# Rotating a matrix by 90 degrees: the last macro tile's outputs as 1024 by 512 blocks, and five loads issued ahead

## The chip, the cores and the metric

One core of one Trainium2 chip. The metric is the device time of one execution in microseconds. A profiled execution also has a span, from its first to its last instruction, which is a little shorter than its device time.

## The reference

```python
x = np.random.randn(8192, 8192).astype(np.float32)
def reference(x, k):        # k = 1
    return np.rot90(x, k)
```

Nothing is calculated. Column c of `x` becomes row 8191 - c of the output: the matrix is transposed and its rows are put in reverse order. 268 MB are read and 268 MB are written.

## The kernel before

The input is cut into 16 macro tiles of 1024 rows (R) by 4096 columns (W). A macro tile is loaded as 8 row tiles (T) of 128 rows by 4096 columns, 2 MB each: loads 8 kk to 8 kk + 7 for macro tile kk, 128 in all. It is stored as 8 outputs (J), 128 in all; output n = 8 kk + j holds the 512 columns of chunk j over all 1024 rows, which are 512 rows by 1024 columns of the result. A store is 2 MB too: each of 128 partitions writes four runs (G = 4) of 1024 floats, 4 KB each.

The way of a row tile:

- SP issues its load (`load`, L143) into a landing buffer. Five buffers take the first loads. From load 8 on two of them are for landing (LAND) and three for outputs (OUTS). SP waits until the load before in the same buffer has been copied away.
- DVE copies it into a ring of 63 chunks (SLOTS), reversing the 512 columns of each chunk on the way (L190). A copy is cut into pieces, because the ring is one chunk smaller than a macro tile: piece by piece it waits for the transposes of the macro tile before (`s_half`, `s_first`). Each piece adds one to `s_rev`.
- PE transposes 128x128 blocks of the ring into PSUM (L219), 32 for one output: four blocks times eight row tiles. PSUM is held as two halves, `ps0` and `ps1`, each of 128 x 2048 floats. The first output of a macro tile goes through its row tiles in order, so that PE can start while loads are still coming; the others go through it block by block.
- ACT copies each half from PSUM to an output buffer (L253) and adds one to `s_ev`, for which PE's next use of that half waits. After the second half it issues the store (L259).

Every engine goes through its list in order. `out_buf(n)` gives the buffer of an output: the three output buffers in turn, but for the last eight outputs the two landing buffers are used too, since no more loads come into them. Output 120 takes the buffer of load 126, output 124 that of load 127, output 125 that of load 126 again. ACT waits until the store before in this buffer has landed, or, where a landing buffer is taken for the first time, until its last load has been copied away.

The five engines' programs stand in a block (`nc.Block()`), one function for each. At the end SP waits for all stores.

Of the kernel before, what the change touches and what calls it, by code (L numbers as in the profile page):

```python
# [6 lines left out]
P = 128  # L7


R = 1024  # L10
T = R // P
W = 4096
G = 4
J = W // (G * P)
# [3 lines left out]
CH = G * P  # L18
F = G * R
SLOTS = T * J - 1  # L20

H = 2
GH = G // H
LAND = 2
OUTS = 3

# [19 lines left out]
def slot(kk, t, j):  # L46

    at = t * J + j if kk % 2 == 0 else J + t + j * T
    return (at + kk // 2 * (J + 1)) % SLOTS


def kernel(tc: tile.TileContext, x: bass.AP, k: bass.AP, out: bass.AP):
    nc = tc.nc
# [3 lines left out]
    N, M = x.shape  # L57
    dt = x.dtype
    macros = [(r0, c0) for r0 in range(0, N, R) for c0 in range(0, M, W)]
    KK = len(macros)  # L60
    n_out = KK * J
    n_load = KK * T
    assert T == J


    order = [(kk, a, b) for kk in range(KK) for a in range(T) for b in range(J)]
    for i, (kk, t, j) in enumerate(order):
        if i >= SLOTS:
# [3 lines left out]
    with tc.tile_critical():  # L72
        ident = nc.alloc_sbuf_tensor("ident", [P, P], dt)
        scratch = nc.alloc_sbuf_tensor("scratch", [P, 1], dt)
        bufs = [nc.alloc_sbuf_tensor(f"buf{i}", [P, F], dt) for i in range(LAND + OUTS)]
        ring = nc.alloc_sbuf_tensor("ring", [P, SLOTS * CH], dt)
        ps = [
            nc.alloc_psum_tensor(f"ps{h}", [P, GH * R], mybir.dt.float32)
            for h in range(H)
        ]  # L80

# [3 lines left out]
        s_rev = nc.alloc_semaphore("s_rev")  # L85
        s_first = nc.alloc_semaphore("s_first")
        s_half = nc.alloc_semaphore("s_half")
        s_ev = nc.alloc_semaphore("s_ev")

        def load_buf(m):  # L90
            return m % (LAND + OUTS) if m < T else m % LAND
# [12 lines left out]
        pieces, rev = {}, {}  # L104
        done = 0
        for m in range(n_load):
            kk, t = divmod(m, T)
            got = []
            if m >= T:
                full = (s_half, H * (m - T + 1))  # L110
                first = (s_first, m - T + 2)
            else:
                full = None
                first = (s_first, 1) if t == T - 1 else None
            cuts = [0, 1, J - 1, J] if t == T - 1 else [0, J - 1, J]
            if m < T - 1:
                cuts = [0, J]
            for lo, hi in zip(cuts[:-1], cuts[1:]):
                got.append((lo, hi, first if hi == J else full if lo == 0 else None))
                done += 1  # L120
                for j in range(lo, hi):
                    rev[m, j] = done
            pieces[m] = got
# [16 lines left out]
        def load(e, m):  # L140
            r0, c0 = macros[m // T]
            b = load_buf(m)
            e.dma_start(  # L143
                out=bufs[b][:], in_=x[r0 + m % T * P : r0 + (m % T + 1) * P, c0 : c0 + W]
            ).then_inc(s_land[b], 16)

        def uses_before(n_or_m, buf):
            return sum(buf(i) == buf(n_or_m) for i in range(n_or_m))

        with nc.Block() as block:  # L150

            @block.gpsimd
            def _(e):
                e.memset(ident[:], 0.0).then_inc(s_id, 1)  # L154
                e.wait_ge(s_id, 1)
                e.affine_select(  # L156
                    out=ident[:],
                    in_=ident[:],
                    compare_op=mybir.AluOpType.not_equal,
                    fill=1.0,  # L160
                    base=0,
                    pattern=[[-1, P]],
                    channel_multiplier=1,
                ).then_inc(s_id, 1)

            @block.sync
            def _(e):
                for m in range(n_load):
                    last = [i for i in range(m) if load_buf(i) == load_buf(m)]
                    if last:  # L170
                        e.wait_ge(s_rev, rev[last[-1], J - 1])
                    load(e, m)
                for b in range(LAND + OUTS):
                    n = sum(out_buf(i) == b for i in range(n_out))
                    if n:
                        e.wait_ge(s_store[b], 16 * n)

            @block.vector
            def _(e):
                for m in range(n_load):  # L180
                    kk, t = divmod(m, T)
                    b = load_buf(m)
                    a = bufs[b][:].rearrange("p (j c) -> p j c", c=CH)
                    e.wait_ge(s_land[b], 16 * (uses_before(m, load_buf) + 1))
                    for lo, hi, wait in pieces[m]:
                        if wait:
                            e.wait_ge(*wait)
                        for j, n, at, step in runs(kk, t, lo, hi):
                            v = ring[:, at * CH : (at + (n - 1) * step + 1) * CH]
                            i = e.tensor_copy(  # L190
                                out=bass.AP(
                                    tensor=v.tensor,
                                    offset=v.offset,
                                    ap=[v.ap[0], [step * CH, n], [1, CH]],
                                ),
                                in_=a[:, j : j + n, ::-1],
                            )
                        i.then_inc(s_rev, 1)

            @block.tensor  # L200
            def _(e):
                seen = {}

                def wait(sem, n):
                    if seen.get(sem, 0) < n:
                        seen[sem] = n
                        e.wait_ge(sem, n)

                e.wait_ge(s_id, 2)
                for n in range(n_out):  # L210
                    kk, j = divmod(n, J)

                    def transpose(t, g):
                        if n:
                            wait(s_ev, H * (n - 1) + g // GH + 1)
                        wait(s_rev, rev[kk * T + t, j])
                        at = slot(kk, t, j) * CH + g * P
                        f = g % GH * R + t * P
                        i = e.transpose(  # L219
                            ps[g // GH][:, f : f + P], ring[:, at : at + P], ident[:]  # L220
                        )
                        if t == T - 1 and g % GH == GH - 1:
                            i.then_inc(s_half, 1)
                        elif t == 0 and g == G - 1:
                            i.then_inc(s_first, 1)

                    if j == 0:
                        for t in range(T):
                            for g in range(G):
                                transpose(t, g)  # L230
                    else:
                        for g in range(G):
                            for t in range(T):
                                transpose(t, g)

            @block.scalar
            def _(e):
                e.wait_ge(s_id, 2)
                e.copy(scratch[:], ident[:, :1])  # L239
                for n in range(n_out):  # L240
                    r0, c0 = macros[n // J]
                    b = out_buf(n)
                    o = bufs[b][:].rearrange("m (g f) -> m g f", g=G)
                    for h in range(H):
                        if h == 0:
                            stores = uses_before(n, out_buf)
                            loads = [i for i in range(n_load) if load_buf(i) == b]
                            if stores:
                                e.wait_ge(s_store[b], 16 * stores)
                            elif loads:  # L250
                                e.wait_ge(s_rev, rev[loads[-1], J - 1])
                        e.wait_ge(s_half, H * n + h + 1)  # L252
                        e.copy(  # L253
                            o[:, h * GH : (h + 1) * GH, :],
                            ps[h][:].rearrange("m (g f) -> m g f", g=GH),
                        ).then_inc(s_ev, 1)
                    top = M - c0 - (n % J + 1) * G * P
                    e.wait_ge(s_ev, H * (n + 1))
                    e.dma_start(  # L259
                        out=out[top : top + G * P, r0 : r0 + R].rearrange(  # L260
                            "(g m) f -> m g f", g=G
                        ),
                        in_=o,
                    ).then_inc(s_store[b], 16)


# [33 lines left out]
```

## Time and profile before

| | |
|---|---|
| device time, median of 3 runs | 1268.4 us (1267.63 to 1268.76) |
| device time of the profiled execution | 1267.9 us |
| its span | 1266.0 us |
| bytes read and written | 268.44 MB each, 424 GB/s over the span |
| one load, issue to landing (median) | 16.8 us |
| one store, issue to landing (median) | 25.7 us |
| one PSUM half copied by ACT (mean) | 1.87 us |

In the profile's rows PE is the matrix engine, DVE the vector engine, ACT the scalar engine, SP the engine that issues the loads; ACTq and SPq are the sequencers of ACT and SP, where DMA issues and waits are seen. A timeline row gives the start, the duration, engine, line, operation, output and input, the number of instructions merged into the row, and in brackets how long the engine had been idle and what ended it. A row of stretches gives for each engine the busy time and the number of instructions, then the clock granted to PE, the mean busy share of the 16 DMA engines and the rate at which they moved data.

### The profile page before, as it was taken

How to read it: one execution, taken by the hardware profiler on the slowest of the kernel's cores; microseconds unless marked ns; L12 is line 12 of the kernel's file. 1: busy time of each engine (PE TensorE's matmuls, PEld its weight loads, DVE VectorE, ACT ScalarE, POOL GpSimd, SP SyncE). 2: the span in 40 equal slices, each digit the busy share in tenths (PEclk: the TensorE clock that was granted, in tenths of full speed). 3: DMA queues.
4: the chain of work that ended last, by engine and by line, in shares of the span. 5: the costliest groups of instructions: out<-in, count | busy, mean ns of one | idle time of the engine just before them, and what ended most of it. 6: DMA issues, size and time to landing. Idle time of an engine off the chain costs nothing.

```text
span 1266.0 us, 9358 instructions
## 1 busy us (share of the span) xinstructions
PE 690.1 (55%) x4096; PEld 639.0 (50%) x4096; DVE 403.2 (32%) x313; ACT 467.8 (37%) x258; POOL 0.7 (0%) x6
## 2 busy tenths in 40 slices
PE   1555555554555445655456556565564655646664
PEld 1544445544455444544445546465464655646554
DVE  3322432234323343232342333432234222442210
ACT  0433334333243342433424334243432434324444
POOL 0000000000000000000000000000000000000000
PEclk9987877768678787786867776777767777677677
DMA  9999999999999999999999999999999999999988
GB/s 398 421 429 430 428 428 428 430 430 429 429 429 429 430 427 429 428 430 429 430 430 428 428 429 430 429 429 429 426 429 428 427 429 427 430 429 427 428 359 374
DMA packets 36904, 537.48 MB, mean 425 GB/s; under 512 B 4096, under 2 KB 4096, under 8 KB 4096
## 3 DMA queue, kind: packets, MB, share of 16 engines
q10 hardware_dynamic: 18432, 268.44, 49.9%
q1 hardware_dynamic: 18432, 268.44, 49.7%
q8 instruction: 32, 0.52, 0.2%
q14 instruction: 8, 0.07, 0.0%
HBM read 268.44 MB, written 268.44 MB: 424 GB/s over the span
## 4 chain that ended last, share of the span: by engine, by line
DMA 81%; issue 9%; DVE 6%; ACT 2%; PE 0%; ACTq 0%; SPq 0%
DMA buf<-in_x_dram 81%; DVE ring L190 6%; ACT buf L253 2%; PE ps L219 0%; ACTq L259 0%; SPq L143 0%; ACTq L252 0%; SPq L295 0%; SPq L72 0%
## 5 line engine op out<-in xcount | busy, mean ns | idle before, releaser
L219 PE MATMUL ps<-ident,ring 128*128 128x128 f32 x4096 | 690.1, 345 | 559.8 <-ACT buf L253 415.0
L219 PEld LDWEIGHTS ps<-ident,ring 128*128 128x128 f32 x4096 | 639.0, 183 | 610.7 <-ACT buf L253 453.8
L253 ACT COPY buf<-ps 128x2048 f32<-128x2048 f32 x256 | 466.4, 1870 | 783.4 <-DMA out_dram<-buf 499.4
L190 DVE COPY ring<-buf 128x512 f32<-128x512 f32 (+7 forms) x313 | 403.2, 1338 | 815.7 <-DMA buf<-in_x_dram 814.0
L239 ACT ACT_TABLE_LOAD x1 | 1.3, 1283 | 0.9 <-SPq L72 0.9
L156 POOL TENSOR_SCALAR_AFFINE_SELECT ident<-ident 128x128 f32<-128x128 f32 x1 | 0.3, 294 | 0.2 <-POOL ident L154 0.2
L154 POOL MEMSET ident<- 128x128 f32 x1 | 0.2, 206 | 0.5 <-SPq L72 0.5
L239 ACT COPY scratch<-ident 128x1 f32<-128x1 f32 x1 | 0.2, 193 | 0.0
L281 POOL MEMSET const-bfloat16-1.0<- 128x1 bf16 x1 | 0.1, 103 | 0.0
L281 POOL MEMSET const-uint8-127<- 128x1 uint8 x1 | 0.1, 103 | 0.0
L281 POOL MEMSET const-float32-0.0<- 128x1 f32 x1 | 0.1, 100 | 0.2 <-issue 0.2
L281 POOL MEMSET const-float32-1.0<- 128x1 f32 x1 | 0.1, 100 | 0.0
## 6 DMA issues: line engine op xcount, KB each, us to landing
buf<-in_x_dram SPq DMA_DIRECT2D x128, 2048.0 KB, 16.8
out_dram<-buf ACTq DMA_DIRECT2D x128, 2048.0 KB, 25.7
```

Of the source, the lines that this page charges most:

```text
L154: e.memset(ident[:], 0.0).then_inc(s_id, 1)
L156: e.affine_select(out=ident[:], in_=ident[:], compare_op=mybir.AluOpType.not_equal, fill=1.0, base=0, pattern=[[-1, P]], channel_multiplier=1,
L190: i = e.tensor_copy(out=bass.AP(tensor=v.tensor, offset=v.offset, ap=[v.ap[0], [step * CH, n], [1, CH]],), in_=a[:, j : j + n, ::-1],)
L219: i = e.transpose(ps[g // GH][:, f : f + P], ring[:, at : at + P], ident[:])
L239: e.copy(scratch[:], ident[:, :1])
L253: e.copy(o[:, h * GH : (h + 1) * GH, :], ps[h][:].rearrange("m (g f) -> m g f", g=GH),).then_inc(s_ev, 1)
L281: nc = _bacc.Bacc("TRN2", target_bir_lowering=False, num_devices=1)
```

## The change

It has two parts. First, the eight outputs of the last macro tile are cut in another way. Each is made of four row tiles and two chunks instead of eight row tiles and one chunk: 1024 rows by 512 columns of the result. The first four need the first four row tiles, the last four the other four. The store has the same 2 MB, but each partition writes eight runs of 512 floats, 2 KB, instead of four of 4 KB. The list `outs` holds, for each output, the macro tile, its row tiles and its chunks, and PE and ACT walk it. The buffers (`out_buf`) stay as they were. Second, SP issues the first five loads before the block of the engines' programs instead of as the first steps of its own program.

```diff
+END = T // 2
...
+    outs = [(kk, range(T), [j]) for kk in range(KK - 1) for j in range(J)]
+    wide = T // END
+    for t in range(0, T, END):
+        for j in range(0, J, wide):
+            outs.append((KK - 1, range(t, t + END), range(j, j + wide)))
...
-            cuts = [0, 1, J - 1, J] if t == T - 1 else [0, J - 1, J]
+            begin = wide if kk == KK - 1 else 1
+            cuts = [0, begin, J - 1, J] if t == T - 1 else [0, J - 1, J]
...
+        for m in range(LAND + OUTS):
+            load(nc.sync, m)
+
         with nc.Block() as block:
...
             @block.sync
             def _(e):
-                for m in range(n_load):
+                for m in range(LAND + OUTS, n_load):
                     last = [i for i in range(m) if load_buf(i) == load_buf(m)]
-                    if last:
-                        e.wait_ge(s_rev, rev[last[-1], J - 1])
+                    e.wait_ge(s_rev, rev[last[-1], J - 1])
                     load(e, m)
...
-                for n in range(n_out):
-                    kk, j = divmod(n, J)
-
-                    def transpose(t, g):
+                for n, (kk, ts, js) in enumerate(outs):
+                    blocks = [(j, g) for j in reversed(js) for g in range(G)]
+                    half = len(blocks) // H
+                    rows = len(ts) * P
+
+                    def transpose(t, b):
+                        j, g = blocks[b]
                         if n:
-                            wait(s_ev, H * (n - 1) + g // GH + 1)
+                            wait(s_ev, H * (n - 1) + b // half + 1)
                         wait(s_rev, rev[kk * T + t, j])
                         at = slot(kk, t, j) * CH + g * P
-                        f = g % GH * R + t * P
+                        f = b % half * rows + (t - ts[0]) * P
...
+                    order = [(t, b) for b in range(len(blocks)) for t in ts]
+                    if js[0] == 0:
+                        order.sort()
+                    for t, b in order:
+                        transpose(t, b)
...
                         e.copy(
-                            o[:, h * GH : (h + 1) * GH, :],
-                            ps[h][:].rearrange("m (g f) -> m g f", g=GH),
+                            bufs[b][:, h * F // H : (h + 1) * F // H], ps[h][:]
                         ).then_inc(s_ev, 1)
-                    top = M - c0 - (n % J + 1) * G * P
+                    top = M - c0 - (js[-1] + 1) * CH
                     e.wait_ge(s_ev, H * (n + 1))
                     e.dma_start(
-                        out=out[top : top + G * P, r0 : r0 + R].rearrange(
-                            "(g m) f -> m g f", g=G
-                        ),
-                        in_=o,
+                        out=out[
+                            top : top + len(js) * CH, r0 + ts[0] * P : r0 + ts[0] * P + rows
+                        ].rearrange("(g m) f -> m g f", m=P),
+                        in_=bufs[b][:].rearrange("m (g f) -> m g f", f=rows),
                     ).then_inc(s_store[b], 16)
```

More of the change, by code (lines that the diff above doesn't have):

```diff
@@ L20 @@
 SLOTS = T * J - 1
+END = T // 2
 H = 2
-GH = G // H
 LAND = 2
@@ L63 @@
     assert T == J
+    outs = [(kk, range(T), [j]) for kk in range(KK - 1) for j in range(J)]
[3 more added lines that the diff above has]
+            outs.append((KK - 1, range(t, t + END), range(j, j + wide)))
+    assert len(outs) == n_out
     order = [(kk, a, b) for kk in range(KK) for a in range(T) for b in range(J)]
@@ L77 @@
         ps = [
-            nc.alloc_psum_tensor(f"ps{h}", [P, GH * R], mybir.dt.float32)
+            nc.alloc_psum_tensor(f"ps{h}", [P, F // H], mybir.dt.float32)
             for h in range(H)
@@ L209, in _ @@
                 e.wait_ge(s_id, 2)
-                for n in range(n_out):
-                    kk, j = divmod(n, J)
-                    def transpose(t, g):
+                for n, (kk, ts, js) in enumerate(outs):
[4 more added lines that the diff above has]
+                        j, g = blocks[b]
                         if n:
-                            wait(s_ev, H * (n - 1) + g // GH + 1)
+                            wait(s_ev, H * (n - 1) + b // half + 1)
                         wait(s_rev, rev[kk * T + t, j])
                         at = slot(kk, t, j) * CH + g * P
-                        f = g % GH * R + t * P
+                        f = b % half * rows + (t - ts[0]) * P
                         i = e.transpose(
-                            ps[g // GH][:, f : f + P], ring[:, at : at + P], ident[:]
+                            ps[b // half][:, f : f + P], ring[:, at : at + P], ident[:]
                         )
-                        if t == T - 1 and g % GH == GH - 1:
+                        if t == ts[-1] and b % half == half - 1:
                             i.then_inc(s_half, 1)
-                        elif t == 0 and g == G - 1:
+                        elif t == ts[0] and b == len(blocks) - 1:
                             i.then_inc(s_first, 1)
[L227 to L234, printed above, removed]
+                    order = [(t, b) for b in range(len(blocks)) for t in ts]
[3 more added lines that the diff above has]
+                        transpose(t, b)
             @block.scalar
@@ L239, in _ @@
                 e.copy(scratch[:], ident[:, :1])
-                for n in range(n_out):
-                    r0, c0 = macros[n // J]
+                for n, (kk, ts, js) in enumerate(outs):
+                    r0, c0 = macros[kk]
+                    rows = len(ts) * P
                     b = out_buf(n)
-                    o = bufs[b][:].rearrange("m (g f) -> m g f", g=G)
                     for h in range(H):
```

## Prediction

> **What bounds the kernel now.** I read the page first, then stretches of the span at its end, then the end in order of time, then landings of single transfers.
>
> ```profile
> span 1266.0 us, 9358 instructions
> PE 690.1 (55%) x4096; PEld 639.0 (50%) x4096; DVE 403.2 (32%) x313; ACT 467.8 (37%) x258; POOL 0.7 (0%) x6
> GB/s 398 421 429 430 428 428 428 430 430 429 429 429 429 430 427 429 428 430 429 430 430 428 428 429 430 429 429 429 426 429 428 427 429 427 430 429 427 428 359 374
> q10 hardware_dynamic: 18432, 268.44, 49.9%
> q1 hardware_dynamic: 18432, 268.44, 49.7%
> q8 instruction: 32, 0.52, 0.2%
> DMA 81%; issue 9%; DVE 6%; ACT 2%; PE 0%; ACTq 0%; SPq 0%
> ```
>
> No compute engine is busy over 55%, the two DMA queues fill the 16 DMA engines, and the rate stands at 426 to 430 GB/s in all slices but the first two and the last two. Every byte is still moved once after the change, so only those slices have something to give. The last two are 69 and 54 GB/s below 428, over 31.65 us each: 2.2 and 1.7 MB, or 9 us together. About 4 us of it are after the last byte, which the change doesn't touch. The rest is here:
>
> ```profile
> 1200.00:1215.00 15.00, 6.13 (x28) 5.27 (x28) 2.62 (x2) 3.63 (x2) 0.00 (x0) 0.67 1.01 428
> 1215.00:1217.00 2.00, 0.44 (x2) 0.45 (x3) 0.93 (x2) 0.00 (x0) 0.00 (x0) 0.50 0.71 303
> 1217.00:1219.00 2.00, 0.67 (x4) 0.27 (x2) 1.83 (x3) 1.67 (x1) 0.00 (x0) 0.50 0.46 197
> 1219.00:1222.00 3.00, 2.74 (x13) 2.75 (x14) 0.00 (x0) 1.97 (x2) 0.00 (x0) 0.50 0.07 27
> 1222.00:1230.00 8.00, 7.16 (x63) 6.65 (x62) 0.00 (x0) 6.66 (x4) 0.00 (x0) 0.99 0.94 391
> 1230.00:1262.00 32.00, 17.60 (x152) 16.20 (x150) 0.00 (x0) 18.82 (x11) 0.00 (x0) 0.86 1.01 425
> 1262.00:1266.00 4.00, 0.00 (x0) 0.00 (x0) 0.00 (x0) 0.00 (x0) 0.00 (x0) 0.50 0.05 20
> ```
>
> The last two columns are the mean DMA share and GB/s. From 1215 to 1222 the engines run dry one by one: full, 0.71, 0.46, 0.07. Summed against 1.01 that is 0.6 + 1.1 + 2.8 = 4.5 us of idle time of the mean engine, and 0.6 us more up to 1230. But 27 GB/s is one sixteenth of 428: from 1219 to 1222 exactly one DMA engine is still at work at full speed. The engines are not abreast, and the slowest hardly stops.
>
> Why the others stop is seen in order of time (numbers of outputs and loads counted from 0; outputs 120 to 127 and loads 120 to 127 are those of the last macro tile):
>
> ```profile
> 1184.20 0.55 ACTq L259 DMA_DIRECT2D out_dram<-buf  x1
> ...
> 1194.03 0.55 ACTq L259 DMA_DIRECT2D out_dram<-buf  x1
> ...
> 1202.10 0.69 PE L219 MATMUL ps<-ident,ring 128*128 128x128 f32 x2 [3.23 <-ACT buf L253]
> 1203.84 0.55 ACTq L259 DMA_DIRECT2D out_dram<-buf  x1
> 1203.86 5.45 PE L219 MATMUL ps<-ident,ring 128*128 128x128 f32 x26 [1.08 <-ACT buf L253]
> 1206.30 2.62 DVE L190 COPY ring<-buf 128x3584 f32<-128x3584 f32 x2 [7.18 <-DMA buf<-in_x_dram]
> 1216.07 2.76 DVE L190 COPY ring<-buf 128x512 f32<-128x512 f32 x4 [7.15 <-DMA buf<-in_x_dram]
> 1217.33 3.64 ACT L253 COPY buf<-ps 128x2048 f32<-128x2048 f32 x2 [13.52 <-PE ps L219]
> 1221.00 0.55 ACTq L259 DMA_DIRECT2D out_dram<-buf  x1
> ...
> 1226.34 0.55 ACTq L259 DMA_DIRECT2D out_dram<-buf  x1
> ...
> 1252.21 0.55 ACTq L259 DMA_DIRECT2D out_dram<-buf  x1
> ```
>
> Store 119 is issued at 1203.84. Output 120 has 28 of its 32 transposes by 1209.3, waits for the last load (reversed from 1216.07), and is issued at 1221.00. No load is left and no store comes for 17 us. The last number of the next rows is the time to landing: of all stores in the median, then of stores 118, 119 and 127 alone.
>
> ```profile
> out_dram<-buf ACTq DMA_DIRECT2D x128, 2048.0 KB, 25.7
> out_dram<-buf ACTq DMA_DIRECT2D x1, 2048.0 KB, 23.9
> out_dram<-buf ACTq DMA_DIRECT2D x1, 2048.0 KB, 19.0
> out_dram<-buf ACTq DMA_DIRECT2D x1, 2048.0 KB, 12.2
> ```
>
> So 118 lands at 1194.03 + 23.9 = 1217.9, 119 at 1203.84 + 19.0 = 1222.8, 127 at 1252.21 + 12.2 = 1264.4. A transfer lands when its slowest DMA engine is through, so 1222.8 is that engine's mark. It comes 0.8 us after store 120 has begun to move (the rate is back at 1222).
>
> **Part one: outputs 120 to 127 take four row tiles each.** Outputs 120 to 123 need only loads 120 to 123. The same 2 MB leave per store, the same 32 transposes of 128x128 and two evictions of 128x2048 are done per output, and the PSUM halves hold as much. What moves is when store 120 can go. Its transposes are no longer held by loads: four may start at 1202.10 and the other 28 with the second half of PSUM free at 1203.86. PE did 26 in 5.45 us there, 0.21 each, so 28 end by 1209.7 and the first half a transpose or so earlier. But the first of these outputs still takes landing buffer 0, which load 126 fills: ACT waits for its reversal, 1206.30 + 2.62 = 1208.9. Both conditions fall together. ACT then needs 3.64 us, so store 120 is issued at about 1212.7 instead of 1221.0, 8.3 us earlier. Data follow an issue by 1.0 us (1221.00 to 1222), so they flow from 1213.7, before the first engine runs dry at 1215. Queued behind ACT's new wait is only ACT's own work, and PE's next output; DVE's last pieces need output 120's first transposes (about 1204.5) and are not held.
>
> What is late next? Output 121 in the same manner costs up to 5.34 us (1226.34 less 1221.00, with PE not yet at speed), so it issues by about 1218.0, and the others follow at ACT's 4.31 us ((1252.21 - 1226.34) / 6). Buffers: 121 takes that of store 117 (issued at 1184.20, landed a median 25.7 later, at 1209.9), 122 that of 118 (1217.9, ACT comes at 1218.6), 123 that of 119 (1222.8, ACT comes at 1222.9). A store takes the 16 engines 2.097 MB / 425 GB/s = 4.93 us, so ACT stays ahead of them and the queue stays filled. Output 124 needs load 127, reversed at 1218.8, long before its turn; 125 to 127 take the buffers of 120 to 122, which land some three stores ahead of that.
>
> With the queue filled, the slowest engine goes on at 1222.8 with eight stores: 8 x 4.93 = 39.5, so the last store lands at 1262.3 instead of 1264.4. **That is 2.1 us**, not the mean engine's 5.1: what faster engines finish early ends nothing.
>
> The trace shows no store with 2 KB runs. Its nearest rows are loads alone (16 KB runs, first row pair) and stores alone (4 KB runs, second pair):
>
> ```profile
> DMA packets 1034, 15.11 MB, mean 432 GB/s; under 512 B 112, under 2 KB 112, under 8 KB 112
> q1 hardware_dynamic: 1034, 15.11, 101.0%
> DMA packets 926, 13.60 MB, mean 425 GB/s; under 512 B 96, under 2 KB 96, under 8 KB 96
> q10 hardware_dynamic: 925, 13.58, 100.8%
> ```
>
> So q1 is the loads, q10 the stores. A row of four runs costs up to 432/425 = 1.6% more than one of one run; by the page's shares it is 49.9 against 49.7, 0.4%. Four runs more instead of three more make 0.5 to 2.2% of 39.5 us: 0.2 to 0.9 us. I exclude a gain from shorter runs: the longer runs are the faster ones in both pairs of rows. I take 0.4, between the two rows; the range goes further, since 2 KB is outside what they cover. The Trainium skill ("Perfetto Trace Analysis", DMA Optimizations) says that small DMAs under 2 KB carry a significant overhead each and that going from 2 KB to 4 KB or 8 KB can improve throughput dramatically. It gives no figure; the rows above agree in direction, with 0.4 to 1.6%, and as a full effect it is the first rival below.
>
> ACT's own issue may grow with the runs (min/median/max in ns, stores and then loads):
>
> ```profile
> L259 ACTq DMA_DIRECT2D out_dram<-buf x128: 546/547/658, 47.4 to 1252.2; - x128
> L143 SPq DMA_DIRECT2D buf<-in_x_dram x128: 327/328/500, 1.0 to 1199.1; - x128
> ```
>
> An issue with four runs per row took 0.547 us on ACT, one with a single run 0.328 on SP. At 0.22 for three runs the four new ones add 0.29; if the issue doubles, 0.55. ACT's pace becomes 4.6 to 4.86 us a store, still under 4.93, so this is hidden behind the stores' own transfers. If that cover were gone, the slowest engine would still have half a dozen stores queued ahead of it, and pays only what is left after those.
>
> **Part two: five loads issued ahead.** SP's start, from the chain of waits:
>
> ```profile
> 0.72 0.01 SPq L72
> 0.74 0.06 issue
> 0.80 0.03 SPq L295
> 0.83 0.12 issue
> 0.96 0.38 SPq L143
> ```
>
> The first load is issued at 0.96, after a branch at 0.80 into SP's program. Ahead of it, the load can come at 0.75 to 0.85: 0.1 to 0.2 us, I take 0.15. The engines are full from the first load on, so it reaches the end whole. The five issues hold SP alone, which has nothing else to do then; DVE needs no one before the first landing.
>
> **Sum.** Profiled execution 1267.9 (span 1266.0 and 1.9 around it): 1267.9 - 2.1 + 0.4 - 0.15 = 1266.05. The median, 1268.4, stands 0.5 above the profiled one, so 1266.5 in its terms.
>
> **The rivals.** (a) Slower: 2 KB runs move slower than the rows let me think. The stores of the last 39.5 us are all on the slowest engine's path, so every per cent costs 0.4 us. The gains of 2.1 and 0.15 us are gone at 2.25 / 39.5 = 5.7%; slower by 0.2% (2.5 us, about what a measurement of this kernel can tell from no change) needs 12%, or 5.5 us a store. At 20%, 7.9 us replace the 0.4: 1274.0. For it: nothing in the trace covers 2 KB. Against it: going from one run to four cost 1.6% at most.
> (b) Faster than forecast: the lag of the one engine is an accident of this execution, or is made up once others are idle. Then the mean engine's idle time counts, 4.5 + 0.6 us: 1268.4 - 5.1 + 0.4 - 0.15 = 1263.5. For it: a lag of 3 us is 0.25% of the span. Against it: the lone engine moved 27 GB/s from 1219 to 1222, its sixteenth and no more.
> (c) The slowest engine has an instruction fetch in the tail. Queue q8 took 0.2% of 16 x 1266 us for 32 packets, 1.3 us each, and the page doesn't say on which engines. Then 1.3 us come back: 1267.8.
> (d) It doesn't do what it says: output 120 is held by something that I take as free, and the dry stretch stays. Then 1268.4 + 0.4 - 0.15 = 1268.7.
>
> **How the numbers follow.** The forecast has 0.49. With the run cost at 0.2 to 0.9 and the slowest engine's mark a little over 1 us earlier or half a microsecond later in other executions (the three times before spread over 1.1 us), it covers 1265.1 to 1267.5. (a) has 0.16, (b) 0.21, (c) 0.10, (d) 0.04. Faster by over 0.2% is below 1265.9: (b) and a third of the forecast, 0.38 rounded up. Slower by over 0.2% is above 1270.9: (a), 0.16. Within 0.2% is the rest, 0.46. The range reaches down past (b) to 1263.3 and up to a run cost of 8% (3.2 us), 1269.3; left out are most of (a) and what of (b) gains more.
>
> **What would show it.** In the profile after: store 120 issued at 1212 to 1213.5, and ACT's eviction before it ended by DVE or PE at about 1209; no stretch between 1213 and 1262 under 0.9 of DMA share, unless faster engines finish early, which the last stretch would show as a share that falls in steps; first load issued at 0.75 to 0.85; stores alone at 415 to 425 GB/s. Wrong if the stores alone run below 400 GB/s (a), if the last stretch ends sharply and 5 us earlier (b), or if a dry stretch stays before 1222 (d).

## The result, and the profile after

Over 22 runs of each, the median is 1266.16 us after and 1268.66 us before: ratio 0.9984, 95% interval 0.9978 to 0.9991. The kernel is faster by 0.16%, about 2 us (2.5 us by the two medians): inside the 0.2% that the prediction called no change, but with an interval that leaves out 1. The profiled execution after took 1266.16 us, its span 1264.2, where before had 1267.9 and 1266.0.

The page after, the lines that answer to those of before:

```profile
span 1264.2 us, 9359 instructions
GB/s 397 423 429 430 429 427 429 429 430 429 428 429 429 430 430 427 427 430 430 428 430 427 429 430 429 427 427 428 429 428 428 427 430 428 428 427 426 427 425 335
q10 hardware_dynamic: 18432, 268.44, 50.0%
q1 hardware_dynamic: 18432, 268.44, 49.8%
q8 instruction: 32, 0.52, 0.2%
```

The last slice but one has risen from 359 to 425 GB/s; the last has fallen from 374 to 335, because engines now finish early there. The stretches at the end (last two columns: mean DMA share, GB/s), first after, then the end of before:

```profile
1213.00:1222.00 9.00, 8.16 (x69) 7.65 (x68) 2.50 (x4) 7.07 (x4) 0.00 (x0) 0.95 1.01 422
1222.00:1230.00 8.00, 5.92 (x42) 5.41 (x41) 0.00 (x0) 3.86 (x3) 0.00 (x0) 0.85 1.00 420
1230.00:1250.00 20.00, 13.13 (x109) 12.05 (x107) 0.00 (x0) 14.55 (x8) 0.00 (x0) 0.93 1.00 415
1250.00:1258.00 8.00, 0.00 (x0) 0.00 (x0) 0.00 (x0) 0.00 (x0) 0.00 (x0) 0.50 0.91 383
1258.00:1260.00 2.00, 0.00 (x0) 0.00 (x0) 0.00 (x0) 0.00 (x0) 0.00 (x0) 0.50 0.30 123
1260.00:1262.00 2.00, 0.00 (x0) 0.00 (x0) 0.00 (x0) 0.00 (x0) 0.00 (x0) 0.50 0.06 25
```

```profile
1260.00:1262.00 2.00, 0.00 (x0) 0.00 (x0) 0.00 (x0) 0.00 (x0) 0.00 (x0) 0.50 0.92 393
1262.00:1264.00 2.00, 0.00 (x0) 0.00 (x0) 0.00 (x0) 0.00 (x0) 0.00 (x0) 0.50 0.10 41
```

The dry stretch from 1215 to 1222 is gone: the share is 1.01. But the idle time has only moved. Before, fourteen of the 16 engines ended together, by 1262.4 (0.92, then 0.10). After, they end one by one, and from 1260 to 1262 a single engine works (25 GB/s, one sixteenth). It decides the time.

The chain that this comes from, in order of time:

```profile
1208.69 3.63 ACT L265 COPY buf<-ps 128x2048 f32<-128x2048 f32 x2 [5.38 <-DVE ring L202]
...
1212.36 0.55 ACTq L270 DMA_DIRECT2D out_dram<-buf  x1
...
1217.94 0.55 ACTq L270 DMA_DIRECT2D out_dram<-buf  x1
...
1222.25 0.94 ACTq L270 DMA_DIRECT2D out_dram<-buf  x1
1223.29 3.63 ACT L265 COPY buf<-ps 128x2048 f32<-128x2048 f32 x2 [1.06 <-DMA out_dram<-buf]
...
1226.95 1.17 ACTq L270 DMA_DIRECT2D out_dram<-buf  x1
...
1231.57 3.64 ACT L265 COPY buf<-ps 128x2048 f32<-128x2048 f32 x2 [4.65 <-PE ps L234]
...
1235.24 0.55 ACTq L270 DMA_DIRECT2D out_dram<-buf  x1
...
1248.17 0.55 ACTq L270 DMA_DIRECT2D out_dram<-buf  x1
```

ACT is released by DVE, the reversal of load 126, and issues store 120 at 1212.36. The landings of stores 119 (issued at 1203.35), 120 and 127:

```profile
out_dram<-buf ACTq DMA_DIRECT2D x1, 2048.0 KB, 19.3
out_dram<-buf ACTq DMA_DIRECT2D x1, 2048.0 KB, 15.3
out_dram<-buf ACTq DMA_DIRECT2D x1, 2048.0 KB, 14.4
```

119 lands at 1222.65, 120 at 1227.66 and 127 at 1262.6. The slowest engine needs 40.0 us for its last eight stores, 5.0 each, without a pause. Before, 1222.8 to 1264.4 were 41.6 us.

The start of SP, from the chain of waits after:

```profile
0.80 0.03 SPq L306
0.83 0.12 issue
0.96 0.38 SPq L153
```

The first load stands at 0.96 us, to the hundredth where it was.

### The profile page after: what moved, and what is told of

Same layout as the page of the kernel before. It is cut to its first block, busy times and chain, and to the rows that moved or that the text cites. A ratio compares the mean times of both kernels' runs of the same rounds, so it can differ in the third digit from the quotient of the medians.

```text
span 1264.2 us, 9359 instructions
## 1 busy us (share of the span) xinstructions
PE 715.5 (57%) x4096; PEld 666.9 (53%) x4096; DVE 402.9 (32%) x313; ACT 467.6 (37%) x258; POOL 0.7 (0%) x6
## 2 busy tenths in 40 slices
DMA packets 36904, 537.48 MB, mean 425 GB/s; under 512 B 4096, under 2 KB 4096, under 8 KB 4096
## 4 chain that ended last, share of the span: by engine, by line
DMA 78%; issue 10%; DVE 5%; ACT 3%; PE 2%; ACTq 0%; SPq 0%
DMA buf<-in_x_dram 77%; DVE ring L202 5%; ACT buf L265 3%; PE ps L234 2%; DMA out_dram<-buf 1%; ACTq L270 0%; SPq L153 0%; ACTq L264 0%; SPq L306 0%; SPq L81 0%
## 5 line engine op out<-in xcount | busy, mean ns | idle before, releaser
L234 PE MATMUL ps<-ident,ring 128*128 128x128 f32 x4096 | 715.5, 353 | 530.3 <-ACT buf L265 394.6
L234 PEld LDWEIGHTS ps<-ident,ring 128*128 128x128 f32 x4096 | 666.9, 188 | 578.7 <-ACT buf L265 433.6
```

The source lines that it names most:

```text
L234: i = e.transpose(ps[b // half][:, f : f + P], ring[:, at : at + P], ident[:])
```

## The experiments

The theory: the end is set by the one DMA engine that lags most, as long as it never runs dry. Rivals: what counts is the idle time of the mean engine (the idle time averaged over the 16); or the gain comes from the outputs' shape. Then the question of why one engine lags at all: the theory there became instruction fetches, which run on the same DMA engines.

Ratios are to the kernel before on the same chip; after has 0.9984. Changes in us are differences of ratios times 1268.

**Holding store 120 back.** Two kernels delay it, by about 10 and by about 6 us.

```diff
 hold_120
-            ends = [load_buf(n_load - 2)]
+            ends = [load_buf(n_load - 1)]
...
-            ends += [load_buf(n_load - 1)]
+            ends += [load_buf(n_load - 2)]
```

> The kernel after, with the two landing buffers exchanged among the last outputs: output 120 takes the buffer of load 127 instead of load 126, so store 120 goes out at about 1222 instead of 1212, as in the kernel before, with 2 KB runs kept. If the end is set by the slowest DMA engine, which works through until 1222 anyway: about 1268 to 1269, that is before plus 0.5 us for the shorter runs. If the idle time of the mean engine counted, the dry stretch of 4.5 us would come back whole: 1270.5 or more. If the gain came from the shape of the outputs and not from the time of store 120: 1266, as after.

```diff
 hold_short
                                 e.wait_ge(s_rev, rev[loads[-1], J - 1])
+                            if n == n_out - J:
+                                e.wait_ge(s_rev, rev[n_load - 1, 0])
```

> The kernel after, but output 120 also waits for the first piece of load 127, about 1216.5, so store 120 is issued at about 1220 and moves from 1221: 7.6 us later than after, but still before the slowest DMA engine is through with store 119 (1222). If the slowest engine sets the end, the delay costs nothing but lost lead of the faster engines, which shows only where an instruction fetch hits one of them: 1266.2 to 1267.2. If the idle time of the mean engine counts, some 3.5 us of it come back: 1269.7.

Measured: hold_120 1270.46 us, ratio 1.0016 (1.0008 to 1.0025); hold_short 1269.16, ratio 1.0006 (0.9997 to 1.0015). So the gain hangs on the time of store 120, not on the shape: with the shape kept and the store late, all of the gain is lost, and in hold_120 2 us more. But both lie closer to the mean engine's number than to the slowest engine's, so I looked for where. In hold_120, store 120 was issued at 1222.95, a microsecond later than I had assumed, and this is what the stretches show:

```profile
1219.00:1222.00 3.00, 0.79 (x4) 0.80 (x5) 0.25 (x1) 2.71 (x2) 0.00 (x0) 0.50 0.23 98
1222.00:1224.00 2.00, 2.00 (x11) 2.00 (x10) 0.00 (x0) 0.92 (x1) 0.00 (x0) 0.50 0.00 0
```

Nothing moves for 2 us: the slowest engine has run dry too, which before it hardly did. This run doesn't tell the theories apart. In hold_short store 120 went out at 1218.66, in time, but another hole came later:

```profile
1239.00:1241.00 2.00, 1.69 (x15) 1.70 (x16) 0.00 (x0) 2.00 (x2) 0.00 (x0) 1.00 0.67 279
1241.00:1243.00 2.00, 2.00 (x19) 1.77 (x17) 0.00 (x0) 1.33 (x2) 0.00 (x0) 1.00 0.62 262
```

Store 124 was issued only at 1241.06. Output 124 is the first of chunks 0 and 1 in its row tiles, so PE takes it row tile by row tile; its first half is then complete only near the end of its 32 transposes, and ACT waits for it (4.65 us after, row above). After covers that with stores still queued; hold_short had too few. The next run takes this hole away.

```diff
 hold_short_blocks: hold_short, and
-                    if js[0] == 0:
+                    if js[0] == ts[0] == 0:
```

> hold_short with output 124 transposed block by block instead of row tile by row tile. In hold_short store 124 came 8.3 us after store 123, because ACT waited 4.65 us for output 124's row by row transposes, and all engines stood idle 2 us before it. If that, and not the 6.3 us later store 120, was the loss against after (the slowest engine was busy all through the hold): 1266.2 to 1267.3. If the idle time of the faster engines at the hold counts: 1268.7 to 1269.2 as hold_short.

Measured 1268.23 us, ratio 1.0001 (0.9992 to 1.001): 0.6 us better than hold_short, with overlapping intervals, and 2.2 above after. Again above what I expected of the slowest engine. Its store 119 (issued at 1203.78) and 127 (issued at 1251.59) landed after

```profile
out_dram<-buf ACTq DMA_DIRECT2D x1, 2048.0 KB, 18.4
out_dram<-buf ACTq DMA_DIRECT2D x1, 2048.0 KB, 12.7
```

that is at 1222.2 and 1264.3. Eight stores of 5.0 us from 1222.2 end at 1262.2; the last engine is 2.1 us later. The stretches say which:

```profile
1260.00:1262.00 2.00, 0.00 (x0) 0.00 (x0) 0.00 (x0) 0.00 (x0) 0.00 (x0) 0.50 0.96 401
1262.00:1264.00 2.00, 0.00 (x0) 0.00 (x0) 0.00 (x0) 0.00 (x0) 0.00 (x0) 0.50 0.04 16
```

All engines work to 1262 side by side, and then one goes on alone. Between 1219 and the end this run has two instruction fetches, as before has:

```profile
q8 instruction: 2, 0.03, 0.3%
```

(the row reads alike in both; in before, from 1222 to 1264, 0.3% of 16 engines' 42 us is 1.0 us each). In hold_short_blocks the faster engines had spent their lead waiting, so all started the last stores abreast, and an engine with a fetch ends behind all others. After, the fetches fall on engines that are microseconds ahead and vanish in that lead. So my theory as written was too simple: the lead of the fast engines isn't worthless, it pays for the fetches. The mean engine's rule isn't right either: by the shares from 1215 to 1222 hold_short_blocks idled 3.1 us in the mean (0.60 and 0.41 over two microseconds each, 0.65 over three), and 1.3 us more before store 121 (0.68 from 1224 to 1226, 0.35 in the microsecond after), and lost 2.2.

The trace also tells which engine a fetch held. Each of the 16 engines closes its share of a transfer with a packet of 4 bytes: there are 4096 packets under 512 B, 16 for each of 256 transfers. So the times of the last 16 say when each engine was through with the last store. In before they lie as follows, from 1262.0 to 1262.5 and from 1262.5 to 1264.2:

```profile
DMA packets 16, 0.03 MB, mean 66 GB/s; under 512 B 14, under 2 KB 14, under 8 KB 14
DMA packets 5, 0.05 MB, mean 29 GB/s; under 512 B 2, under 2 KB 2, under 8 KB 2
```

Fourteen engines end by 1262.4, one at 1263.5 and one at 1264.0. Followed back from store to store, these two fall behind the others just where the two fetches stand, at 1227.8 and 1246.8. Such a fetch takes about 1.0 us, and the data packet right behind it another 1.0 instead of 0.6: the engine loses 1.4 us (median of 29 fetches). In hold_short_blocks fifteen engines end by 1262.5, and the sixteenth, at 1263.8, falls behind at its fetch at 1246.3. In after, from 1256.3 to 1256.6 and from 1260.1 to 1263, it is otherwise:

```profile
DMA packets 12, 0.08 MB, mean 273 GB/s; under 512 B 7, under 2 KB 7, under 8 KB 7
DMA packets 4, 0.05 MB, mean 17 GB/s; under 512 B 1, under 2 KB 1, under 8 KB 1
```

Seven engines end by 1256.6, eight between 1258.5 and 1260.0, the last at 1262.2. From 1217.1 on, that last engine closes a store every 4.98 to 5.06 us, so neither of the two fetches of this stretch (1220.9 and 1242.1) fell on it.

**Fewer and more fetches.** If the lag is made of fetches, PE's program is the place: the q8 rows have 32 fetches of 16 KB, 0.52 MB, for 4096 transposes.

```diff
 quarter_transposes (after), quarter_before (before, the same in its loop)
                     for t, b in order:
+                        if n and t not in (ts[0], ts[-1]):
+                            continue
                         transpose(t, b)
```

> The kernel after, but PE transposes only the first and the last row tile of each output (from output 1 on), so most of the output is stale data; all loads, copies and stores are as they were. PE's program shrinks to about a quarter, and with it the instruction fetches on the DMA engines, from 32 to about 9. If the lag of the slowest DMA engine is made of such fetches, unequally spread over the engines: its lag behind the others at the end shrinks from some 3 to 6 us to under 3, and the time falls by 3 to 6 us, to 1260 to 1263. If the lag is that engine's own, or noise of the transfers, or if fetches are spread evenly and hidden: 1265.5 to 1266.5, and the DMA share in the last stretch falls in steps as before.

> The kernel before with PE transposing only the first and the last row tile of each output (from output 1 on), as quarter_transposes does with after; most of the output is stale data. The instruction fetches fall to about 8 here too. If what the change gains is the idle time that unequal fetches cause at the end, nothing is left for it to gain: 1260 to 1261.5, within 1 us of quarter_transposes. If the gain doesn't depend on the fetches: 2.4 us above quarter_transposes, 1263.

Measured: quarter_transposes 1260.59 us, ratio 0.9939 (0.9927 to 0.9951), 5.7 us less than after; quarter_before 1259.33, ratio 0.9927 (0.9914 to 0.9939). Both pages have

```profile
q8 instruction: 8, 0.13, 0.0%
```

and the end of quarter_transposes is

```profile
1252.00:1254.00 2.00, 0.00 (x0) 0.00 (x0) 0.00 (x0) 0.00 (x0) 0.00 (x0) 0.50 0.82 344
1254.00:1255.00 1.00, 0.00 (x0) 0.00 (x0) 0.00 (x0) 0.00 (x0) 0.00 (x0) 0.50 0.36 147
1255.00:1256.00 1.00, 0.00 (x0) 0.00 (x0) 0.00 (x0) 0.00 (x0) 0.00 (x0) 0.50 0.08 33
```

By the closing packets the engines end within 2.9 us of one another (1252.9 to 1255.8), where after they took 5.8 (1256.4 to 1262.2). The same 268 MB in and out go 5.7 us faster, though no load, copy or store was touched. With a quarter of the fetches the change gains nothing: the kernel before has the lower ratio, with overlapping intervals. This is the clearest answer to what the change is worth: it takes back end time that unequal engines lose. Its own price, the shorter runs, remains.

Packets laid end to end (on one engine, a packet starts some 3 ns before the one before it has ended) say how the 32 fetches of after are spread: about four each on half of the engines, and none on the seven that end first. Packets of nearly the same time can be mistaken for one another in this, so it is a reconstruction. Three fetches fewer on each of eight engines, at 1.4 us, are 4.2 of the 5.7 us; the rest isn't accounted for.

PE's work fell with its program too (24% busy at a granted clock of 0.985, against 57% at 0.73 after), so the other direction was tried on an engine that has nothing to do, GpSimd, with a control.

```diff
 more_fetches (pool_few: a tile of 128 x 256, five memsets, each waiting for the one before)
+                for n in range(n_out):
+                    e.wait_ge(s_ev, H * (n + 1))
+                    if n:
+                        e.wait_ge(s_sp, 64 * n)
+                    for c in range(64):
+                        e.memset(spare[:, c : c + 1], 0.0).then_inc(s_sp, 1)
```

> The kernel after with 64 tiny memsets more on GpSimd for each output, 8192 in all, which touch nothing that the kernel uses. GpSimd's program grows by about as much as PE's program has, so the instruction fetches double from 32 to about 64. If each fetch holds up its DMA engine by some 1.3 us and the engine with most of them sets the end: 2.7 us (spread evenly) to 7 us (piled up as before) more, 1269 to 1273. If fetches are hidden: 1266.

> A control for more_fetches: after with five memsets of 128x256 on GpSimd per output, 640 in all instead of 8192, so GpSimd writes for a similar time but its program stays small (about 5 to 12 more instruction fetches instead of 66). If the 38 us of more_fetches came from the fetches, all on few DMA engines: 1266 to 1272. If they came from GpSimd's work beside VectorE, whose copies were 10% slower there: 1290 to 1305.

Measured: more_fetches 1304.49 us, ratio 1.0291 (1.0276 to 1.0305), 39 us more than after and far above what I expected; pool_few 1268.09, ratio 0.9994 (0.9985 to 1.0003), 1.3 us more, with overlapping intervals. The fetches of more_fetches, and then of pool_few, are in another queue than PE's:

```profile
q14 instruction: 74, 0.60, 0.1%
L210 DVE COPY ring<-buf 128x512 f32<-128x512 f32 (+7 forms) x313 | 444.9, 1469 | 810.1 <-DMA buf<-in_x_dram 810.1
```

```profile
q14 instruction: 14, 0.11, 0.0%
L210 DVE COPY ring<-buf 128x512 f32<-128x512 f32 (+7 forms) x313 | 405.2, 1344 | 817.6 <-DMA buf<-in_x_dram 814.9
```

66 fetches of 8 KB more cost 39 us, 0.6 us each; six more cost 1.3, which can't be told from nothing. That is what they would cost if all ran on one engine, whose lag outgrows the queued work of the others: the page's slices of more_fetches swing between 386 and 430 GB/s. The packets laid end to end bear this out as far as they can be followed, to 360 us: all 16 GpSimd fetches between 50 and 360 us lie on one engine, which has by then moved 14 packets of 16 KB, 8.6 us, less than an engine without a fetch. From there on most engines run dry once in each macro tile, every 81 us, by 0.3 to 1.6 us in the mean. Such a fetch takes 0.31 us, and the packet behind it 0.90 instead of 0.61: 0.6 us again. The control is incomplete all the same: GpSimd wrote for 210 us in pool_few and 282 in more_fetches, and DVE's copies were slower by 0.6% there and 10% here. DVE isn't what ends the wait in either (it waits for loads 810 us), so I take the fetches to be the cause; whether DVE's slower copies add to the 39 us isn't shown.

**The price of runs.** Stores of all outputs in runs of 2 KB and of 16 KB, and the last outputs in runs of 1 KB:

```diff
 all_runs_2k (of before)
-                        out=out[top : top + G * P, r0 : r0 + R].rearrange(
-                            "(g m) f -> m g f", g=G
-                        ),
-                        in_=o,
+                        out=out[
+                            M - c0 - (n % J // 2 + 1) * 2 * CH : M - c0 - n % J // 2 * 2 * CH,
+                            r0 + n % 2 * R // 2 : r0 + (n % 2 + 1) * R // 2,
+                        ].rearrange("(g m) f -> m g f", m=P),
+                        in_=bufs[b][:].rearrange("m (g f) -> m g f", f=R // 2),
 all_runs_16k (of before, the same lines replaced)
+                        out=out[n * 64 : (n + 1) * 64, :].rearrange("r (a f) -> (r a) f", a=2),
+                        in_=bufs[b][:],
 runs_1k (of after)
-END = T // 2
+END = T // 4
```

> The kernel before, with each of the 128 stores written as eight runs of 2 KB per partition to blocks of 1024 by 512 (so chunks land in other places of the output); the same bytes, buffers and order. If shorter runs cost a DMA engine 0.06 us a store (the step between store landings after, 4.98, against 4.92 before): 128 x 0.06 = 7.7 us more, 1276. If they cost only where stores run alone, at the end: 0.5 us more, 1269. If 2 KB is in the range where small transfers lose much: over 1290.

> The kernel before, with each store written as one run of 16 KB per partition (64 whole rows of the output, so the data lie in other places). If the cost is one of runs, 0.015 us for each run that a partition has more: three runs fewer give 128 x 0.045 = 5.8 us less, 1262.8. If four runs of 4 KB cost nothing over one: 1268.5.

> The kernel after with END = 2: the last macro tile's outputs are of two row tiles by four chunks, 2048 by 256 of the result, in runs of 1 KB. Store 120 still waits for load 126's buffer. A packet of 16 KB took a DMA engine 0.611 us as one run, 0.615 as four, 0.625 as eight; if sixteen runs take 0.64 to 0.66, eight stores are 1 to 2 us longer than after: 1267 to 1268. If the cost of runs stays that of 2 KB: 1266.

Measured: 2 KB 1280.3 us, ratio 1.0092 (1.0078 to 1.0106); 16 KB 1267.99, ratio 1.0002 (0.9991 to 1.0012); 1 KB at the end 1271.1, ratio 1.0018 (1.0009 to 1.0027). So four runs a row cost nothing that can be measured over one; eight cost 11.7 us for 128 stores, 0.09 us a store (0.08 to 0.11). Sixteen cost much more than I expected. The rate from 1233 to 1253, where stores run alone, of before (4 KB), after (2 KB) and runs_1k (1 KB):

```profile
DMA packets 584, 8.54 MB, mean 427 GB/s; under 512 B 63, under 2 KB 63, under 8 KB 63
```

```profile
DMA packets 573, 8.34 MB, mean 417 GB/s; under 512 B 64, under 2 KB 64, under 8 KB 64
```

```profile
DMA packets 518, 7.59 MB, mean 379 GB/s; under 512 B 55, under 2 KB 55, under 8 KB 55
```

2.3% less, then 9% less again: 40 us of stores become 4.0 us longer, which is the 4.3 us that runs_1k is above after. Quartering the last outputs pays more for its runs than halving gains.

**What else the change holds.** One run without the loads ahead, and one with only the first two outputs in the new shape:

```diff
 two_wide
     for t in range(0, T, END):
-        for j in range(0, J, wide):
-            outs.append((KK - 1, range(t, t + END), range(j, j + wide)))
+        outs.append((KK - 1, range(t, t + END), range(wide)))
+    outs += [(KK - 1, range(T), [j]) for j in range(wide, J)]
```

```diff
 outputs_only
-        for m in range(LAND + OUTS):
-            load(nc.sync, m)
...
-                for m in range(LAND + OUTS, n_load):
+                for m in range(n_load):
                     last = [i for i in range(m) if load_buf(i) == load_buf(m)]
-                    e.wait_ge(s_rev, rev[last[-1], J - 1])
+                    if last:
+                        e.wait_ge(s_rev, rev[last[-1], J - 1])
```

> The kernel after without its second part: the five loads are issued as first steps of SP's own program again. In the trace of after the first load still starts at 0.96 us, as before, so the loads ahead bring nothing: ratio to before 0.998 as after has it, first load at 0.96. If they had brought the 0.15 us forecast, no time could show it, but the first load of after would stand at 0.8.

> The kernel after with only two outputs in the new shape, 120 (first four row tiles of chunks 0 and 1) and 121 (the other four), and outputs 122 to 127 in the old one with 4 KB runs. Store 120 goes out at 1212 as after; store 121 waits for load 127 and goes out at about 1222.5, when only the slowest engine has work left. By the slowest engine: six stores at 0.08 to 0.1 us less, 0.5 us less than after, 1265.7. By the mean engine: a dry stretch of some 2 us before store 121 comes back, 1267.5 to 1268.

Measured: outputs_only 1266.13 us, ratio 0.9983 (0.9974 to 0.9992), first load at 0.96: the second part of the change does nothing. two_wide 1265.76, ratio 0.9982 (0.9973 to 0.999): the forecast 0.5 us lies within the interval and can't be told from nothing, but the 1267.5 to 1268 of the mean engine's rule, 0.9995 and more, lie outside it. In its dry stretch before store 121 the faster engines idled,

```profile
1219.00:1222.00 3.00, 1.59 (x15) 1.60 (x16) 0.00 (x0) 3.00 (x2) 0.00 (x0) 1.00 0.83 350
1222.00:1224.00 2.00, 2.00 (x20) 1.86 (x18) 0.00 (x0) 1.33 (x2) 0.00 (x0) 1.00 0.75 303
```

and it cost nothing that can be measured: here the slowest engine was busy, and enough lead was left. Of the versions that compute the whole result, none beat the changed kernel by more than its noise.

## Why the prediction was right

The forecast was 1266.5 us, the median 1266.16; in the profiled execution it was -1.85 us and came to -1.7, with -1.8 in the span. Path and number held for the kernel after. For the kernel before, the account of its end was wrong in part, and some of the agreement is luck. By its steps:

- Store 120 at about 1212.7, released at 1208.9 by load 126's reversal: issued at 1212.36, ACT released by DVE at 1208.69. Store 121 by 1218.0: 1217.94. ACT at output 123 just when store 119 lands: it came at 1223.2, store 119 had landed at 1222.65. (The 1.06 us in its row are no wait for that landing: 0.94 of them are its own issue of store 122.) All as worked out.
- The slowest engine goes on at its mark and decides: last landing forecast 1262.3, with the run cost 1262.7; measured 1262.6. Share falling in steps at the end: so it was. Rival (b), 5.1 us from the mean engine, fell with this. That no fetch fell on the slowest engine in its last 40 us the prediction had no reason for; it had left rival (c) a chance of 0.10.
- The run cost, taken as 0.4: all_runs_2k gives 0.09 us a store, 0.7 for eight, inside the bounds of 0.2 to 0.9. The step of 5.0 instead of 4.93 between landings gives 0.6. The straight line through one and four runs was the wrong way to reach it: nothing to four, 2% to eight, 11% to sixteen. The Trainium skill ("Perfetto Trace Analysis", DMA Optimizations) says that small DMAs, under 2 KB, have a significant overhead and that going from 2 KB to 4 KB or 8 KB can improve throughput dramatically. For runs within a DMA of 2 MB this case bears it out in direction only, with 2.3% lost at 2 KB and 9% more at 1 KB.
- The loads ahead, -0.15: this step failed. The branch still stands at 0.80 and the first load behind it at 0.96. The prediction took this branch for the entry into SP's program of the block; but in after it stands ahead of loads that are issued before the block.
- Not foreseen: output 124's row by row order, 4.65 us of ACT's time, hidden behind queued stores; ACT's issue of two stores stretched to 0.94 and 1.17 us, hidden too. The steady 0.55 of the others, and the 0.55 to 0.66 of all stores in all_runs_2k, say that eight runs alone don't lengthen the issue, against the 0.29 I had allowed.
- Rival (c) was nearly the mechanism, but on the other side. Its price of 1.3 us for a fetch in the tail was right in size (1.4 measured), and it was the kernel before that paid it. The prediction took the engine that lagged at 1222 for the one that ends last in before too. By the packets, all 16 engines of before start store 120 within 0.15 us, from 1222.2 to 1222.35; so there the lag was used up, and the engine that ended last was one that a fetch held at 1246.8. Of the 2.1 us, up to 0.4 are the gap before store 121 (store 120 is through at 1227.1 on the first engine, data flow again at 1227.55), and some 1.7 are what the last engine ended behind the first fourteen. The sum came out because it starts from the slowest engine's mark, which holds for after, and takes the end of before as measured, whatever made it.
- Why an engine lags at all, the prediction had left open as an accident; quarter_transposes and the packets showed that the instruction fetches make most of it.

## What to carry to other kernels

When a kernel is bound by its DMA engines, ask for the slowest of them, not for the mean: a share that falls in steps, or a rate of one sixteenth, shows one engine still working while the sum says idle. Idle time of the others is worth something only as a lead that later delays can be charged to; where all have run dry they start abreast, and the next delay of any of them sets the end. So work out what the last engine does from its last landing on. And an engine's program can be a DMA load of its own: look at the instruction queues before blaming the data.

## What the hardware showed beyond that

Instruction fetches of 0.4 MB (24 of 32) beside 537 MB of data, 0.07%, cost 5.7 us of 1266, 0.45%. Each costs its engine 1.4 us; spread evenly over 16 engines, 24 of them would be 2.1 us. Fetches for GpSimd's program cost 0.6 us each, against 0.2 for PE's ((1266.2 - 1260.6) / 24), although one of PE's is twice as long: GpSimd's lie on one engine, as far as the packets can be followed, and PE's on about eight. Splitting 16 KB of a partition into four runs of 4 KB was free, into eight of 2 KB 2%, into sixteen of 1 KB 11%; at 1 KB ACT's issue of a store reached

```profile
1221.86 2.39 ACTq L270 DMA_DIRECT2D out_dram<-buf  x1
```

where it takes 0.55 at 4 KB. Of the eight stores in 1 KB runs the first took 0.55 us too, and the seven behind it 0.7 to 2.4; all_runs_2k stayed at 0.55 to 0.66. So the length of the runs alone doesn't make it; how much the stores queued ahead do isn't shown.
